# One place for each of the last steps of an RWKV kernel: the order of the last fourteen pairs and last four groups written out

## The chip, the cores and the metric

The kernel runs on one core of one Trainium2 chip. The metric is the device time of one execution in microseconds (us).

## The reference

The reference is the RWKV "wkv" recurrence over `k` and `v` of shape 16 x 2048 x 256 (batch, time, channel), with a decay `w` and a bonus `u` per channel:

```python
for b in range(batch):
    aa = bb = 0;  pp = -1e38
    for t in range(seq_len):
        ww = u + k[b, t];  qq = max(pp, ww)
        e1 = exp(pp - qq);  e2 = exp(ww - qq)
        output[b, t] = (e1 * aa + e2 * v[b, t]) / (e1 * bb + e2 + 1e-08)
        ww = pp - w + k[b, t];  qq = max(ww, k[b, t])
        e1 = exp(ww - qq);  e2 = exp(k[b, t] - qq)
        aa = e1 * aa + e2 * v[b, t];  bb = e1 * bb + e2;  pp = qq
```

So each output is a weighted sum of all earlier values divided by the sum of the weights.

## The kernel before

**Tiling.** Time is cut into 16 groups of 128 steps, and the batch into 4 portions of 4 rows. One *pair* is one portion of one group, a tile of 128 time steps by 4 rows by 256 channels; pair `n` belongs to group `c = n // 4`, and there are 64 pairs. Inside a pair the 128 steps are two halves of 64. The state at the start of each half is carried for a whole group at once.

**What is done for pair n.** Each of these is a *step* with a name:

- `LK`, `LV`: loads of k and v (512 KB each), issued by GpSimd (POOL), the first three pairs by SyncE (SP). `RK` casts k to the matmul's format, `CV` casts v to bf16. `RK` is on VectorE (DVE) for three pairs of four and on POOL for the fourth; `CV` is on POOL from pair 10 on.
- `R q n` and `L q n` (q is 0 or 1): TensorE (PE) matmuls that write decay terms (from `WU`, made of w and u by step `wu`) and then the k term into one of two PSUM tiles `X0`, `X1`. `X q n`: ScalarE (ACT) takes the exponential of the tile into a ring of 11 pairs (`EZR`).
- `TV`: DVE multiplies the exponentials by v. `S`: PE adds up each half's sums into `TOT`.
- `DEN`: PE builds the denominator in an `X` tile. `LN`: ACT takes its logarithm (scaled) into `rd`; `INV`: ACT takes exp(-x) of it in place, which gives the inverse. `NUM`: PE builds the numerator, in its own PSUM tile `num`, and in an `X` tile for odd pairs from 57 on. `MUL`: DVE multiplies both into `ot`. `ST` and `SQ`: stores, on SP and (from pair 52 on, one piece) POOL; the last piece of pair 63 on ACT.

**What is done for group c.** `CS` copies the sums (DVE), `TU` turns them by matmul (PE), `SL` takes logarithms (ACT), `FR` and `OF` make frames and offsets (DVE), `SW` makes weights (ACT), `CH` and `SS` run the recurrence over the halves and spread it (DVE), `TK` turns the states back (PE), `BK` copies them out as `cb` (DVE); `SN` and `KP` hand over to the next group (DVE). `DEN` and `NUM` of the group's pairs need `BK`.

**What sets the order.** Each step gets a *place*, a number: for pair n it is n plus an offset from the table `P` (with separate tables for the last ten pairs' outputs, for the first and the last group's states). `AT` overrides places by name; `mats` makes four small matrices and `wu` the rows of w and u. A loop then takes, again and again, the step with the smallest place whose predecessors (`after`) have been recorded and whose buffer (`take`) is free, and records its instructions:

```python
    todo = sorted(ops, key=lambda x: ops[x]["place"])
    while todo:
        for name in todo:
            o = ops[name]
            if all(x not in ops or "done" in ops[x] for x in o["after"]) and (xs if o["take"] == "X" else free.get(o["take"], 1)):
                break
```

This happens when the program is built; on the chip each engine runs its own instructions in the order in which they were recorded, and waits on semaphores for the others. The two `X` tiles are handed out by the same loop: a step that takes `"X"` (`R`, `DEN`, odd `NUM` at the end) gets the tile that has been free longest. PE also records fillers: `zeros(m)` writes m small matmuls into the tile `TURN` ahead of certain steps (one ahead of each `L`, one ahead of `TU`, four ahead of `TK`; more in the first group). Buffers that count here: 2 of `vb` (from `CV` to `TV`), 2 of `rd` (from `LN` to `MUL`), 1 of `num`, 4 each of `kr` and `vr`, 5 of `kf`, 8 of `ot`.

Of the kernel before, what the change touches and what calls it, by code (L numbers as in the profile page):

```python
# [15 lines left out]
def kernel(  # L16
# [45 lines left out]
         "Z0": {"L": 1, "S": 3, "DEN": 0, "NUM": 6, "TK": 47, "TU": 17, "R": 12},  # L62
         "Z": {"DEN": 0, "L": 1, "NUM": 0, "TK": 4, "S": 0, "TU": 1, "R": 0}}

    AT = {"INV 55": 69.0, "SL 15": 69.1, "LN 56": 69.2, "SW 15": 75.7, "FR 15": 69.3}

    consts = ctx.enter_context(tc.tile_pool(name="consts", bufs=1))
    kpool = ctx.enter_context(tc.tile_pool(name="kpool", bufs=NK))
# [18 lines left out]
    def matrix(name, dt):  # L87
        return consts.tile([128, 128], dt, tag=name, name=name)
# [89 lines left out]
    mats = {name: matrix(name, BF16) for name in ("Id", "IdN", "S", "SN")}  # L178
# [11 lines left out]
    X = [psx.tile([128, 2, D], F32, tag=f"X{a}", name=f"X{a}") for a in range(2)]  # L190
# [31 lines left out]
    AS, D1, L1, A0, FR, BC, A2 = range(7)  # L222
# [88 lines left out]
    RD, NUM, OT = {}, {}, {}  # L311
# [66 lines left out]
    def step(name, place, fn, args=(), after=(), take=None, give=(), mode=0):  # L378
        key = name if isinstance(name, str) else " ".join(map(str, name))
        ops[name] = dict(place=AT.get(key, place), fn=fn, args=args, after=list(after), take=take, give=give, mode=mode)  # L380

# [109 lines left out]
```

## Time and profile before

| | |
|---|---|
| median of 3 runs | 289.46 us (288.67 to 289.91) |
| the profiled execution: time | 289.2 us |
| its span, first to last instruction | 287.5 us |
| busy share of the span | PE 94%, ACT 90%, DVE 86%, POOL 61% |
| granted TensorE clock, mean | 0.995 |
| HBM read and written | 67.12 MB and 33.55 MB, 350 GB/s over the span |

The profile is one execution of the program. Its timeline lists start and duration of instructions per engine in us from the span's start, and in brackets the idle time of the engine before them with what ended it. PEld is the loading of matmul weights. In a group of rows "L210" is line 210 of the kernel; "x4" says that four instructions are merged.

### The profile page before, as it was taken

What the parts mean: (1) busy time and instruction counts of PE and PEld (TensorE: products, weight loads), DVE (VectorE), ACT (ScalarE), POOL (GpSimd) and SP (SyncE); (2) the same over time, 40 slices, a digit from 0 to 9 for tenths busy, and PEclk for the clock granted to TensorE, in tenths of its full rate; (3) what the DMA queues carried; (4) which work ended last, traced back from release to release, by engine and by line L of the source; (5) the groups of instructions that cost most, each with busy time, mean ns of one, the idle gap of its engine ahead of it and who ended that gap; (6) DMA issues with size and microseconds to landing.
All of it is one profiled execution on the core that took longest, in us unless ns stands there. A gap on an engine that the chain in (4) does not pass through costs nothing.

```text
span 287.5 us, 8058 instructions
## 1 busy us (share of the span) xinstructions
PE 271.6 (94%) x3263; PEld 139.2 (48%) x3263; DVE 246.9 (86%) x422; ACT 258.6 (90%) x291; POOL 176.4 (61%) x219
## 2 busy tenths in 40 slices
PE   7989999999999999999999999999999999998860
PEld 6535744454545545454545545454545545454530
DVE  4685879989897979989898989989898989889861
ACT  1776399999999999999999999999999999998991
POOL 8256458575767687575767687575767685421320
PEclk9999999999999999999999999999999999999997
DMA  6999999999999999999999999999999999985896
GB/s 206 348 354 346 347 348 313 384 369 390 374 394 381 383 393 372 391 382 393 355 392 388 389 387 382 394 385 395 370 380 374 389 394 387 347 237 177 235 278 179
DMA packets 58669, 101.20 MB, mean 352 GB/s; under 512 B 5152, under 2 KB 43688, under 8 KB 58632
## 3 DMA queue, kind: packets, MB, share of 16 engines
q0 software_dynamic: 21200, 65.42, 65.5%
q1 hardware_dynamic: 37280, 35.14, 36.4%
q8 instruction: 25, 0.41, 0.6%
q10 hardware_dynamic: 152, 0.14, 0.1%
q14 instruction: 12, 0.10, 0.1%
HBM read 67.12 MB, written 33.55 MB: 350 GB/s over the span
## 4 chain that ended last, share of the span: by engine, by line
PE 81%; ACT 6%; DMA 4%; DVE 4%; issue 2%; SPq 1%; DVEq 0%; ACTq 0%
PE X L207 20%; PE X L323 15%; PE num L323 12%; PE X L201 12%; PE TURN L149 11%; PE TOT L246 7%; DMA ot<-in_v_dram 4%; ACT rd L335 3%; PE TOT L259 2%; DVE ot L355 2%; ACT rd L340 2%; DVE EZR L219 1%; ACT EZR L210 1%; PE TURN L303 1%; SPq L115 1%
## 5 line engine op out<-in xcount | busy, mean ns | idle before, releaser
L210 ACT ACTIVATE EZR<-X 128x1024 bf16<-128x1024 f32 x128 | 126.9, 1014 | 14.4 <-PE X L207 14.2
L214 POOL CAST vb<-vr 128x1024 bf16<-128x1024 f32 x54 | 56.4, 1044 | 69.3 <-DVE EZR L219 67.5
L219 DVE TENSOR_TENSOR EZR<-EZR,vb 128x2048 bf16<-128x2048 bf16 x64 | 77.8, 1219 | 0.4 <-ACT EZR L210 0.2
L355 DVE TENSOR_TENSOR ot<-num,rd 128x1024 f32<-128x1024 f32 x60 | 73.3, 1221 | 3.9 <-ACT rd L340 3.6
L340 ACT ACTIVATE rd<-rd 128x1024 f32<-128x1024 f32 (+1 forms) x65 | 68.0, 1046 | 2.0
L335 ACT ACTIVATE rd<-X 128x1024 f32<-128x1024 f32 (+1 forms) x65 | 65.8, 1012 | 2.3 <-PE X L323 0.7
L149 PE MATMUL TURN<-Z 128*128 128x192 bf16 x319 | 55.2, 259 | 1.4 <-DVE Z L133 1.4
L201 PE MATMUL X<-WU,CO 64*64 64x512 bf16 x512 | 51.9, 390 | 0.9 <-DVE WU L176 0.6
L149 PEld LDWEIGHTS <-Z 128*128 128x128 bf16 x319 | 28.4, 100 | 48.6 <-issue 47.1
L115 POOL DMA_DIRECT2D vr<-in_v_dram x61 | 46.3, 759 | 6.7 <-DVE vb L214 5.9
L207 PE MATMUL X<-kr,NLE 128*128 128x512 f32 x128 | 45.6, 438 | 0.0
L207 PE MATMUL X<-kr,NLZ 128*128 128x512 f32 x128 | 45.5, 437 | 0.0
L108 POOL DMA_DIRECT2D kf<-in_k_dram x53 | 40.1, 756 | 0.0
L194 DVE CAST kr<-kf 128x1024 fp32r<-128x1024 f32 x39 | 31.6, 839 | 4.0 <-DMA kf<-in_k_dram 4.0
L201 PEld LDWEIGHTS <-CO 64*64 64x64 bf16 x512 | 15.7, 105 | 31.1 <-issue 26.3
L323 PE MATMUL X<-EZR,S 64*64 64x512 bf16 x256 | 26.2, 394 | 1.7 <-ACT rd L335 1.0
L323 PE MATMUL X<-cb,Id 64*64 64x512 bf16 x256 | 25.9, 376 | 0.0
L323 PE MATMUL X<-EZR,Id 64*64 64x512 bf16 x256 | 25.9, 376 | 0.0
L323 PE MATMUL num<-EZR,SN 64*64 64x512 bf16 x240 | 24.3, 386 | 1.1 <-DVE ot L355 1.1
L246 PE MATMUL TOT<-EZR,OH 128*32 128x256 bf16 x512 | 23.7, 277 | 1.3 <-DVE EZR L219 1.3
L323 PE MATMUL num<-cb,IdN 64*64 64x512 bf16 x240 | 24.0, 376 | 0.0
L323 PE MATMUL num<-EZR,IdN 64*64 64x512 bf16 x240 | 23.9, 376 | 0.0
(69 smaller groups left out, 269.3 us busy)
## 6 DMA issues: line engine op xcount, KB each, us to landing
vr<-in_v_dram POOLq DMA_DIRECT2D x61, 512.0 KB, 7.7
kf<-in_k_dram POOLq DMA_DIRECT2D x53, 512.0 KB, 8.5
out_dram<-ot SPq DMA_DIRECT2D x64, 256.0 KB, 10.0
out_dram<-ot SPq DMA_DIRECT2D x116, 128.0 KB, 10.1
kr<-in_k_dram POOLq DMA_DIRECT2D x8, 512.0 KB, 8.8
ot<-in_k_dram SPq DMA_DIRECT2D x3, 512.0 KB, 5.9
ot<-in_v_dram SPq DMA_DIRECT2D x3, 512.0 KB, 10.0
out_dram<-ot POOLq DMA_DIRECT2D x11, 128.0 KB, 3.4
```

What stands on the lines that cost most here:

```text
L115: K((SP if n < BYSP else POOL).dma_start(out=vr, in_=rows_of(v, n)))
L149: K(PE.matmul(TURN[:, 0:192], Z[:, 0:128], Z, start=first, stop=True, skip_group_check=True))
L201: K(PE.matmul(X[a][o:o + HS, i, :].rearrange("p (n d) -> p n d", n=2), CO[r:r + HS, q, :], WU[r:r + HS, :].unsqueeze(1).broadcast_to([HS, ...
L207: K(PE.matmul(X[a][:, i, :], (NLE, NLZ)[q], km[:, i, :], start=False, stop=True, skip_group_check=True))
L210: K(SC.activation(ez(n)[:, q, 1], X[a], ACT.Exp))
L214: K((DVE if n < EARLY else POOL).tensor_copy(vb, VR.pop(n)))
L219: K(DVE.tensor_mul(ez(n)[:, :, 0], ez(n)[:, :, 1], vb.unsqueeze(1).broadcast_to([128, 2, 2, D])))
L246: K(PE.matmul(t[32 * j:32 * j + 32, 0:256], OH[:, s:s + 32], ez(n)[:, 0, 1 - q, i, 256 * x:256 * x + 256], start=p == 0 and x == 0, stop=p ...
L323: K(PE.matmul(out_tile[o:o + HS, i, :], left, right, start=s == 0, stop=s == 2, tile_position=(r, o), skip_group_check=True))
L335: K(SC.activation(RD[n][:, i], X[a][:, i], ACT.Ln, scale=RS))
L340: K(SC.activation(RD[n][:, i], RD[n][:, i], ACT.Exp, scale=-1.0))
L355: K(DVE.tensor_mul(o.rearrange("p (i n) d -> p i (n d)", i=2)[:, i], NUM[n][:, i], RD[n][:, i]))
```

## The change

`AT`, which held five places (`INV 55`, `SL 15`, `LN 56`, `SW 15`, `FR 15`), now holds a place for every `R`, `L`, `X`, `TV`, `S`, `DEN`, `LN`, `INV`, `NUM` and `MUL` of pairs 50 to 63, for every state step of groups 12 to 15, and for `mats` and `wu`. Loads, casts and stores (`LK`, `LV`, `RK`, `CV`, `ST`, `SQ`) keep the places that `P` gives, though they can be recorded earlier or later as their predecessors are.

```diff
-    AT = {"INV 55": 69.0, "SL 15": 69.1, "LN 56": 69.2, "SW 15": 75.7, "FR 15": 69.3}
+    AT = {"R 0 50": 48.908, "L 0 50": 39.3462, "X 0 50": 45.2, "R 1 50": 43.3225, "L 1 50": 41.2788,
+          "X 1 50": 48.01, "TV 50": 51.2875, "S 50": 52.283, "DEN 50": 59.8517, "LN 50": 51.2544, "INV 50": 58.126,
...
+          "MUL 63": 73.9425, "mats": -3.08, "wu": -10.79}
```

The instructions are the same in number and kind. What the places come to is an order on each engine. On PE, from the first difference on (fillers left out, order before on the left, after on the right):

```
before                                       after
TK 11 DEN 42 S 50 NUM 42                     TK 11 DEN 42 NUM 42
R,L 53  S 51  DEN 43 NUM 43                  R,L 53  S 50 S 51  DEN 43 NUM 43
R,L 54  TU 12 DEN 44 NUM 44                  R,L 54  TU 12 DEN 44 S 52 S 53 NUM 44
R,L 55  S 52 S 53  DEN 45 NUM 45             R,L 55  DEN 45 NUM 45
R,L 56  TK 12 DEN 46 S 54 NUM 46             R,L 56  TK 12 S 54 DEN 46 NUM 46
R,L 57  S 55  DEN 47 NUM 47                  R,L 57  DEN 47 S 55 NUM 47
R,L 58  TU 13 DEN 48 NUM 48                  R,L 58  TU 13 DEN 48 NUM 48
R,L 59  S 56 S 57  DEN 49 NUM 49             R,L 59  DEN 49 NUM 49
R,L 60  TK 13 DEN 50 S 58 NUM 50             R,L 60  TK 13 DEN 50 DEN 51 S 56 to S 59 NUM 50
R,L 61  S 59  DEN 51 NUM 51                  R,L 61  TU 14 DEN 52 NUM 51
R,L 62  TU 14 DEN 52 NUM 52                  R,L 62  NUM 52
R,L 63  S 60 S 61  DEN 53 DEN 54 NUM 53      R,L 63  DEN 53 DEN 54 NUM 53 S 60 S 61
TK 14 DEN 55 NUM 54 S 62 S 63 TU 15          TK 14 DEN 55 NUM 54 S 62 S 63 TU 15
DEN 56 NUM 55 DEN 57 NUM 56 DEN 58 NUM 57    DEN 56 NUM 55 DEN 57 DEN 58 NUM 56 NUM 57
TK 15 NUM 58 DEN 59 DEN 60 NUM 59 ...        TK 15 DEN 59 NUM 58 NUM 59 DEN 60 ...
```

On ACT, `SW 11` and `SW 13` move ahead of `X 0 51` and `X 0 59`; `LN 51` and `INV 51` move ahead of `X 0 61`; `SW 14` follows `X 1 62`; `SL 15` moves ahead of `INV 55`. On DVE, `TV 53`, `TV 59` and `TV 62` move up to stand right behind `TV 52`, `TV 58` and `TV 61`; `MUL 44` stands ahead of `TV 54`, `CS 14` ahead of `MUL 50`, `TV 63` ahead of `BK 14`, `MUL 56` ahead of `SS 15`; at the start `wu` and `mats` stand ahead of `RK 0` (before: `RK 0`, `wu`, `RK 1`, `RK 2`, `CV 0`, `TV 0`, `CV 1`, `mats`). On POOL, `CV 55` moves ahead of `RK 55`, and `CV 59` ahead of `LK 63`. SP's order is unchanged. From pair 59 on all `DEN`s get `X0` and the odd `NUM`s `X1`.

42 rows, old and new, of the table AT are left out of this document.

## Prediction

> **What bounds the kernel now.** I read the page, then busy time by stage, then ScalarE's (ACT's) waits, then the timelines of the start and the end. Steps are named as in the code: X is the exponential (L210), LN and INV are L335 and L340, R and L the matmuls that fill X (L201, L207), S the sums (L246), DEN and NUM L323, TV L219, MUL L355, CV and RK the casts L214 and L194, and SL, SW, TU, CS, TK, BK, CH, SS the state steps. The page's engine line:
> ```profile
> PE 271.6 (94%) x3263; PEld 139.2 (48%) x3263; DVE 246.9 (86%) x422; ACT 258.6 (90%) x291; POOL 176.4 (61%) x219
> ```
> Two groups of four pairs, and the stage behind them, as windows (us, then busy per engine in the order PE, PEld, DVE, ACT, POOL):
> ```profile
> 212.00:228.00 16.00, 15.96 (x201) 7.98 (x197) 14.70 (x25) 15.75 (x19) 11.36 (x13) 1.00 1.04 382
> 228.00:244.00 16.00, 15.97 (x201) 7.92 (x197) 15.02 (x25) 15.75 (x19) 10.01 (x12) 1.00 1.05 392
> 244.00:260.00 16.00, 15.56 (x207) 7.59 (x200) 13.71 (x24) 15.72 (x19) 4.76 (x5) 1.00 0.91 290
> ```
> PE and ACT are both full: PE has fillers (L149) in its queue, ACT has about 0.25 us of gaps in 16. They are coupled by the two X tiles, since each R, DEN and odd NUM waits for the ACT step that empties its tile. All of ACT's waits that the profile counts:
> ```profile
> ACT EZR L210 <- PE X L207: 14.2, 12, 4.4
> ...
> ACT U L263 <- PE TOT L259: 1.5, 2, 0.8
> ACT rd L335 <- PE X L323: 0.7, 2, 0.5
> ```
> The first row lies before 40 us. Near the end one hole is left, at SL 15 and LN 56:
> ```profile
> 261.88 1.06 ACT L340 ACTIVATE rd<-rd 128x1024 f32<-128x1024 f32 x1
> 263.61 0.28 ACT L263 ACTIVATE U<-TOT 128x128 f32<-128x128 f32 x1 [0.67 <-PE TOT L259]
> 264.40 1.03 ACT L335 ACTIVATE rd<-X 128x1024 f32<-128x1024 f32 x1 [0.51 <-PE X L323]
> ```
> From there ACT starts an LN each 2.00 us until 278.76, and MUL 63 and the last stores follow. The end is thus set by when ACT gets through its queue. The most that any order can win is about 0.4 us in each of the three groups changed (a period is 16.18, from LN 42 at 212.23 to LN 46 at 228.42; the ACT steps placed end to end at the spacings below give 15.7) and some 0.3 of the hole.
>
> **The change, part by part.** No instruction is added or removed; only the order on PE, DVE, ACT and POOL differs, first at the start, then from SW 11 (207.1 us) on. I follow it with spacings, start to start, read from the timeline of 200 to 260 us. PE: R, L, R, L with fillers 2.02, DEN 0.65 (0.77 in front of an S), NUM 0.65, S 0.33 (0.22 before another S), TU 0.62; from the last L to DEN over TK 1.28; a result is there 0.71 after L's start, 0.84 after DEN's. ACT: LN to INV 1.05, INV to next 0.96, X to next 0.91, SW 0.26, SL 0.16. Hand-over 0.05.
>
> *Start.* Making WU and the four small matrices (wu, mats) now stands ahead of RK 0 on DVE:
> ```profile
> 5.07 0.71 DVE L194 CAST kr<-ot 128x1024 fp32r<-128x1024 f32 x1 [0.67 <-DMA ot<-in_k_dram]
> 5.96 0.29 DVE L175 CAST WU<-WUf 128x256 bf16<-128x256 f32 x1 [0.17 <-DMA WUf<-in_u_dram]
> 6.29 0.48 DVE L176 SCALAR_TENSOR_TENSOR WU<-WU,low,WUf 128x256 bf16<-128x256 bf16 x1
> ```
> wu still waits for u (5.96) and ends at 6.77, mats takes 0.74 (its row: 13.79 to 14.53), RK 0 runs from 7.43 to 8.14. L 0 0 starts at 8.19 instead of 7.21, and so PE and ACT run 0.98 late up to S 1. There PE stands anyway, for TV 1 behind v2's transfer:
> ```profile
> 18.13 0.40 PE L246 MATMUL TOT<-EZR,OH 128*32 128x256 bf16 x6 [0.86 <-DVE EZR L219]
> ```
> S 0 would start at 17.75, S 1 at 17.97, still before 18.13: cost 0. The loads k5 to v6, which POOL issues when PE frees a k tile, go 0.98 later, but the DMA runs at 340 to 365 GB/s from 6 to 30 us with transfers queued (k5 is issued at 12.46 and lands at 19.98), so their landings should hold. If this cover were gone, the start costs up to 1.0.
>
> *SW before X (groups 11 and 13).* SW 11 first puts X 0 51 at 206.45 (0.25 late), so DEN 41 starts at 207.51 instead of 207.26, LN 41 at 208.40 (+0.14), LN 42 at 212.39 (+0.16). S 50, moved behind L 1 53, then lets that L end 0.3 earlier, X 1 53 no longer waits, and LN 43 comes at 216.35 (before 216.36): sum 0.
>
> *Sums.* S 52 and S 53 move ahead of NUM 44: NUM 44 at 220.74 (220.09), X 0 55 at 222.52, DEN 45, which waits for that X, and LN 45 +0.14. S 54 moves from behind DEN 46 to ahead of it:
> ```profile
> 227.13 0.39 PE L303 MATMUL TURN<-Id,CB 128*128 128x128 bf16 x4
> 227.53 0.41 PE L323 MATMUL X<-EZR,S 64*64 64x512 bf16 x4
> ...
> 228.30 0.40 PE L246 MATMUL TOT<-EZR,OH 128*32 128x256 bf16 x8
> ```
> LN 46 hangs on DEN 46, so it comes at 228.79 (228.42, +0.37). S 55 moves behind DEN 47, which waits for X 0 57 (ends 231.81): PE stands 0.6 and does S 55 afterwards. NUM 47 comes 0.64 late, LN 48 at 237.18 (236.53, +0.65). SW 13 ahead of X 0 59 holds DEN 49 to 240.51: LN 49 at 241.40 (+0.77), LN 50 at 245.40 (+0.80).
>
> *DEN 51 directly behind DEN 50.* ACT does LN 50 and LN 51 in one run while PE does S 56 to S 59; the waits before X 1 61 (0.1) and LN 51 (0.2) go. SL 14 comes at 251.24; before, the same set of ACT steps ended at 250.76: +0.48. L 0 63 and L 1 63 then come a little late: X 1 63 at 256.66 (255.92, +0.74).
>
> *Tail.* From X 1 63: LN 53 257.58, INV 53 258.63, MUL 53 259.72, TV 63 (now ahead of BK 14) 260.86, S 63 262.13, CS 15 262.59, TU 15 263.07, SL 15 263.79. SL 15 now stands ahead of INV 55, so ACT idles 1.2 in one place, not 0.67 and 0.51 in two. LN 56 at 264.91 (+0.51), LN 57 267.04. LN 58 waited for MUL 56 (268.64); MUL 56, now ahead of SS 15, ends at 268.75, before ACT is ready: LN 58 at 269.05 (268.74, +0.31). All DENs from 59 on share one X tile; each starts 0.05 after the LN that frees it and is done 0.84 later, in the 0.98 that INV takes: still 2.00 per pair. Stores follow unchanged.
>
> *Casts.* TV 53 now directly follows TV 52, so POOL's CV 54 (waits for TV 52's end) runs beside it; CV 55 comes ahead of RK 55 and waits for v55 (landed 219.18). What a collision costs:
> ```profile
> 216.90 1.04 POOL L214 CAST vb<-vr 128x1024 bf16<-128x1024 f32 x1 [0.52 <-DVE EZR L219]
> 217.88 1.50 POOL L194 CAST kr<-kf 128x1024 fp32r<-128x1024 f32 x1
> ```
> RK 55 took 1.50 beside DVE's RK 56 (0.99); alone the two kinds take 1.04 and 0.68. So CV 55 ends near 220.25 and RK 55 between 221.3 (alone) and 221.75; L 0 55 would start at 221.77. If CV 55 too is stretched by 0.46, PE waits 0.45. Bounds 0 to 0.45, and I take 0.15, nearer to the row with one stretch. LK 58, LV 57 and LK 59 go 2 us later; their data had 3.4 us and more to spare before first use.
>
> **Sum.** 0 + 0.31 + 0.15 = +0.45 us. The profiled execution took 289.20 (span 287.5 and 1.7 around it): 289.65; the median of the runs lies 0.26 higher, so 289.9.
>
> **Rivals.** *POOL's casts against TV (slower).* If CV 54 (216.90) gets ahead of TV 53 (216.75) and holds it for its 1.04, TV 53 ends at 219.15, CS 12 starts at 219.06, TU 12 at 219.55 (218.80), MUL 43 ends between 221.6 and 222.05, and NUM 44 comes 0.9 to 1.35 late, on PE and not hidden. With 0.31: +1.2 to +1.65, near 291.1; with v55 another 0.8 late, 291.9. For it: stretched casts are in the trace. Against: TV 53 should be first by 0.15. It decides at which of the two starts first. The Trainium skill (SBUF — State Buffer, "Who interferes with whom") says that a VectorE op with two SBUF inputs and a GpSimd op that reads SBUF exclude each other for the whole instruction; by it the later one loses the full duration, not the 0.3 to 0.5 of the rows. The stretches agree with it, and no row shows a TV beside a POOL cast.
>
> *Start not covered (slower).* TV 1 or the landings slip too: +0.31 and +1.0, near 290.8 to 290.9. Against it: 0.16 us of slack by the rows above.
>
> *The sums cost nothing (faster).* If ACT runs end to end through the three groups, 1.2 is won there and 0.2 to 0.3 at LN 58: 288.0 to 288.3. For it: fewer waits at LN 51 and LN 58. Against it: PE is as full as ACT, and S 54 stands in front of a DEN on which ACT waits already.
>
> **Chances.** Forecast 0.42, POOL's casts 0.35, start 0.09, sums free 0.14. Counting 0.5% (1.45 us, about what a measurement of this kernel can tell from no change): slower 0.31 from the casts, 0.04 from the start, 0.03 from the forecast's upper edge, 0.38; faster 0.08, from the low half of the last case; same 0.54. The range leaves out about 0.1 on each side: 288.2 to 291.9; the forecast's own range is 289.5 to 290.3.
>
> **What would show it.** Right: LN 43 near 216.4 and then LN 46, LN 48 and LN 50 later by 0.4, 0.7 and 0.8; PE idle before DEN 47 and DEN 49; ACT idle over 1 us at SL 15; S 1 again at 18.1. Wrong: S 1 later than 18.2 (start), TV 53 starting after 217 or L 0 55 after 222 (casts), X 1 63 before 255.9 (sums free), or LNs further apart than 2.00 in the tail (the one X tile).

## The result and the profile after

The changed kernel takes 291.00 us (median of 17 runs, 289.86 to 291.76), the kernel before 289.46 in the same job (17 runs, 288.60 to 290.06). The ratio is 1.0044, 95% interval 1.0031 to 1.0057: 1.27 us longer (0.90 to 1.65). The two medians lie 1.54 apart, inside that interval; the ratio is what this text goes by, here and for every experiment. The profiled execution, 289.86 us with a span of 288.1, is the lowest of the 17, so the trace alone shows less than the loss: 0.66 us against the profiled execution before.

In the changed kernel every line number is 44 higher (X is L254, LN and INV L379 and L384, R and L L245 and L251, S L290, DEN and NUM L367, TV L263, MUL L399, CV and RK L258 and L238, SL L307). The engine line of its page, and the three windows shown of before (columns as there, the DMA share and GB/s last):
```profile
PE 271.4 (94%) x3263; PEld 140.3 (49%) x3263; DVE 248.8 (86%) x422; ACT 258.8 (90%) x291; POOL 177.8 (62%) x219
```
```profile
212.00:228.00 16.00, 15.65 (x199) 8.23 (x193) 15.83 (x24) 15.45 (x19) 11.86 (x13) 1.00 1.04 354
228.00:244.00 16.00, 14.81 (x174) 6.92 (x166) 14.48 (x25) 15.50 (x18) 9.16 (x12) 1.00 1.04 391
244.00:260.00 16.00, 15.66 (x214) 8.28 (x214) 13.42 (x24) 15.84 (x19) 7.09 (x6) 1.00 0.80 275
```
ACT's busy time falls from 15.75 to 15.45 and 15.50 in the first two windows and rises from 15.72 to 15.84 in the third. So ACT has about 0.3 us more of gaps in each of the two groups where the S move, and 0.1 less in the one where DEN 51 joins DEN 50. PE, which was full, now stands 0.35 and 1.2 (S 56 and S 57, 0.65 of work, have moved from the second window to the third).

ACT's waits, and the hole near the end, as they are after:
```profile
ACT EZR L254 <- PE X L251: 14.4, 13, 5.3
...
ACT U L307 <- PE TOT L303: 2.0, 2, 1.2
ACT rd L379 <- PE X L367: 0.3, 2, 0.2
```
```profile
261.79 1.01 ACT L379 ACTIVATE rd<-X 128x1024 f32<-128x1024 f32 x1
263.98 0.28 ACT L307 ACTIVATE U<-TOT 128x128 f32<-128x128 f32 x1 [1.18 <-PE TOT L303]
264.15 1.05 ACT L384 ACTIVATE rd<-rd 128x1024 f32<-128x1024 f32 x1
265.10 1.02 ACT L379 ACTIVATE rd<-X 128x1024 f32<-128x1024 f32 x1
```
The two holes of 0.67 and 0.51 have become one of 1.18 at SL 15, and LN 56 starts at 265.10 (264.40).

The trace can be cut at ACT's steps. LN 40 (204.17 before, 204.24 after) stands ahead of every moved step but the start's. From there:

| stretch | before | after | change | predicted |
|---|---|---|---|---|
| LN 40 to LN 42 | 8.06 | 8.19 | +0.13 | +0.16 |
| LN 42 to LN 44 | 8.12 | 7.95 | -0.17 | -0.16 |
| LN 44 to LN 46 | 8.07 | 8.72 | +0.65 | +0.37, casts +0.15 |
| LN 46 to LN 48 | 8.11 | 8.31 | +0.20 | +0.28 |
| LN 48 to LN 50 | 8.07 | 8.19 | +0.12 | +0.15 |
| LN 50 to X 1 63 | 11.32 | 11.22 | -0.10 | -0.06 |
| X 1 63 to LN 56 | 8.48 | 8.28 | -0.20 | -0.23 |
| LN 56 to LN 58 | 4.34 | 4.13 | -0.21 | -0.20 |
| LN 58 to the end of INV 63 | 12.41 | 12.39 | -0.02 | 0 |
| sum | 76.98 | 77.38 | +0.40 | +0.46 |

On ACT's path of this execution the sum was right to 0.06. The runs are longer by 1.27. The experiments ask for the other 0.9 (1.27 less 0.40), and whether the terms above are what the blocks of the change cost.

### The profile page after: what moved, and what is told of

It reads as the page before. It is cut to its first block, busy times and chain, and to the rows that moved or that the text cites. A ratio compares the mean times of both kernels' runs of the same rounds, so it can differ in the third digit from the quotient of the medians.

```text
span 288.1 us, 8060 instructions
## 1 busy us (share of the span) xinstructions
PE 271.4 (94%) x3263; PEld 140.3 (49%) x3263; DVE 248.8 (86%) x422; ACT 258.8 (90%) x291; POOL 177.8 (62%) x219
## 4 chain that ended last, share of the span: by engine, by line
PE 72%; ACT 17%; DVE 4%; issue 2%; DMA 1%; POOL 0%; DVEq 0%; POOLq 0%
PE X L251 18%; PE X L367 14%; PE num L367 11%; PE TURN L193 11%; PE X L245 10%; ACT rd L379 6%; PE TOT L290 6%; ACT EZR L254 5%; ACT rd L384 5%; PE TOT L303 2%; DVE ot L399 1%; DMA WUf<-in_u_dram 1%; DVE EZR L263 1%; PE TURN L347 1%; DVE kr L238 1%
## 5 line engine op out<-in xcount | busy, mean ns | idle before, releaser
L254 ACT ACTIVATE EZR<-X 128x1024 bf16<-128x1024 f32 x128 | 126.5, 1014 | 14.5 <-PE X L251 14.4
L258 POOL CAST vb<-vr 128x1024 bf16<-128x1024 f32 x54 | 59.1, 1096 | 69.6 <-DVE EZR L263 67.1
L399 DVE TENSOR_TENSOR ot<-num,rd 128x1024 f32<-128x1024 f32 x60 | 73.2, 1220 | 5.9 <-ACT rd L384 3.3
L263 DVE TENSOR_TENSOR EZR<-EZR,vb 128x2048 bf16<-128x2048 bf16 x64 | 77.5, 1218 | 0.4 <-ACT EZR L254 0.2
L384 ACT ACTIVATE rd<-rd 128x1024 f32<-128x1024 f32 (+1 forms) x65 | 68.0, 1046 | 2.0
L379 ACT ACTIVATE rd<-X 128x1024 f32<-128x1024 f32 (+1 forms) x65 | 65.7, 1011 | 2.0 <-PE X L367 0.3
L245 PE MATMUL X<-WU,CO 64*64 64x512 bf16 x512 | 51.9, 390 | 0.5 <-DVE WU L220 0.2
L251 PE MATMUL X<-kr,NLE 128*128 128x512 f32 x128 | 45.6, 438 | 0.8 <-DVE kr L238 0.8
L251 PE MATMUL X<-kr,NLZ 128*128 128x512 f32 x128 | 45.5, 437 | 0.0
L238 DVE CAST kr<-kf 128x1024 fp32r<-128x1024 f32 x39 | 32.8, 870 | 4.5 <-DMA kf<-in_k_dram 4.5
L245 PEld LDWEIGHTS <-CO 64*64 64x64 bf16 x512 | 15.9, 104 | 30.8 <-issue 25.8
L367 PE MATMUL X<-EZR,S 64*64 64x512 bf16 x256 | 26.2, 395 | 4.0 <-ACT rd L379 2.0
L367 PE MATMUL X<-cb,Id 64*64 64x512 bf16 x256 | 25.9, 376 | 0.0
L367 PE MATMUL X<-EZR,Id 64*64 64x512 bf16 x256 | 25.9, 375 | 0.0
L367 PE MATMUL num<-EZR,SN 64*64 64x512 bf16 x240 | 24.3, 385 | 0.5 <-DVE ot L399 0.4
L367 PE MATMUL num<-cb,IdN 64*64 64x512 bf16 x240 | 24.0, 376 | 0.0
L367 PE MATMUL num<-EZR,IdN 64*64 64x512 bf16 x240 | 24.0, 376 | 0.0
L290 PE MATMUL TOT<-EZR,OH 128*32 128x256 bf16 x512 | 22.6, 276 | 0.2 <-ACT U L307 0.2
```

What stands on the lines that cost most here:

```text
L245: K(PE.matmul(X[a][o:o + HS, i, :].rearrange("p (n d) -> p n d", n=2), CO[r:r + HS, q, :], WU[r:r + HS, :].unsqueeze(1).broadcast_to([HS, ...
L251: K(PE.matmul(X[a][:, i, :], (NLE, NLZ)[q], km[:, i, :], start=False, stop=True, skip_group_check=True))
L254: K(SC.activation(ez(n)[:, q, 1], X[a], ACT.Exp))
L258: K((DVE if n < EARLY else POOL).tensor_copy(vb, VR.pop(n)))
L263: K(DVE.tensor_mul(ez(n)[:, :, 0], ez(n)[:, :, 1], vb.unsqueeze(1).broadcast_to([128, 2, 2, D])))
L367: K(PE.matmul(out_tile[o:o + HS, i, :], left, right, start=s == 0, stop=s == 2, tile_position=(r, o), skip_group_check=True))
```

## Experiments: the start and two blocks

Theories. 1: the order of pairs 50 to 63 on PE and ACT costs what the table shows, and the start nothing. 2: the start isn't covered in most executions. 3: the loss is made by the casts and at S 52 and S 53. Orders are shown as lists of steps on one engine.

**The change without its start.**
```diff
 DVE, changed kernel
-wu  mats  RK 0  RK 1  RK 2  CV 0  TV 0  CV 1
+RK 0  wu  RK 1  RK 2  CV 0  TV 0  CV 1  mats
```


> The change without its start: WU and the four small matrices are made after RK 0 and after CV 1 again, everything from pair 50 on as changed. The changed kernel took 1.0044 of the time before. Theory 1 (the start costs nothing, the whole loss lies in the order of pairs 50 to 63): 1.0040 to 1.0050, about 290.7 on a kernel before of 289.46. Theory 2 (in most executions the start is not covered and costs 0.7 to 1.0 us; the profiled execution of the changed kernel was one with an early v2): 1.0010 to 1.0020, about 289.9.

Measured: 1.0039 (1.0023 to 1.0054). That is theory 1's time: without its start the kernel is 0.15 us faster, give or take 0.59, so a start of 0.7 to 1.0 is ruled out, but not one of half that. The trace says more. PE's timeline at S 0 and S 1 (L290) and the R behind them, of the changed kernel:
```profile
17.66 0.62 PE L290 MATMUL TOT<-EZR,OH 128*32 128x256 bf16 x16
18.21 0.41 PE L245 MATMUL X<-WU,CO 64*64 64x512 bf16 x4
```
and of this one:
```profile
17.01 0.39 PE L290 MATMUL TOT<-EZR,OH 128*32 128x256 bf16 x8
17.34 0.41 PE L245 MATMUL X<-WU,CO 64*64 64x512 bf16 x4
```
Before, S 1 stood 0.86 for TV 1 and this R came at 18.46. With the same start it comes at 17.34 here, and nothing waits: v2 landed earlier (TV 1 at 15.41, before 16.86).

**The changed start alone, in the kernel before.** The same two lines of DVE's list, the other way round.

> The kernel before with the changed start alone. Theory 1: 1.0000, within 0.1%, and S 1 at 18.1 us as before. Theory 2: 1.0025 to 1.0035, 290.2 to 290.5, with S 1, L 0 5 and all that follows later by what the end is later. Both theories want the same S 1 if v2 lands at 16.25 us as in the profile before; they differ where v2 lands earlier.

Measured: 1.0026 (1.0008 to 1.0043), 0.75 us longer. S 0 and S 1 run from 17.99 without a wait and R follows at 18.55. Theory 1 fails, since 1.0000 lies outside the interval: the start does cost.

**S 52, S 53, TV 53 and CV 55 back.**
```diff
 PE, changed kernel
-R,L 54  TU 12  DEN 44  S 52 S 53  NUM 44  R,L 55  DEN 45
+R,L 54  TU 12  DEN 44  NUM 44  R,L 55  S 52 S 53  DEN 45
 DVE
-TV 52  TV 53  CS 12  RK 56  MUL 43  FR 12  OF 12  SN 12
+TV 52  CS 12  RK 56  MUL 43  FR 12  OF 12  SN 12  TV 53
 POOL
-CV 54  CV 55  RK 55
+CV 54  RK 55
```


> The changed kernel with one block undone: TV 53 behind SN 12 again, CV 55 behind RK 55 and its loads, S 52 and S 53 behind L 1 55. Theory 1 (S 52 and S 53 ahead of NUM 44 cost 0.14, the casts 0.15): 0.3 us less than the changed kernel, 1.0034, LN 46 near 228.7. Theory 3 (casts and the S 52 that waits cost all that LN 45 is late, 0.53): 0.5 us less, 1.0027, LN 45 near 224.45. If the block pays for itself later (TV 53 early relieves VectorE): no less, 1.0044.

Measured: 1.0043 (1.0028 to 1.0058). LN 44 to LN 45 takes 4.09 as before (changed kernel 4.59), but LN 45 to LN 46 takes 4.48 (4.13), so that LN 46 gains only 0.15. From LN 40 to the end of INV 63 it is 77.24: 0.14 is won, less than theory 3 wants. In the runs nothing is won (0.03 us, give or take 0.57), as if the block paid for itself later; that interval doesn't rule out theory 1's 0.3 or theory 3's 0.5.

**S 54, S 55, DEN 47 and TV 54 back.**
```diff
 PE, changed kernel
-R,L 56  TK 12  S 54  DEN 46  NUM 46  R,L 57  DEN 47  S 55  NUM 47
+R,L 56  TK 12  DEN 46  S 54  NUM 46  R,L 57  S 55  DEN 47  NUM 47
```


> The changed kernel with another block undone: TV 54 behind SS 12 again, S 54 behind DEN 46, S 55 ahead of DEN 47. Theory 1 (these two places cost 0.37 and 0.28 at LN 46 and LN 48): 0.4 to 0.6 us less than the changed kernel, 1.0025 to 1.0030, LN 46 near 228.8 and LN 48 near 236.8. Theory 3 (the loss is made at pairs 52 and 53 and by the casts): 1.0040, LN 48 no earlier than 237.2.

Measured: 1.0015 (0.9996 to 1.0033), with 77.04 from LN 40 to the end of INV 63: 0.34 won in the trace, 0.84 in the runs (give or take 0.65). LN 44 to LN 46 takes 8.55, LN 46 to LN 48 takes 8.12. So the two blocks overlap: S 52 and S 53 alone make LN 46 late by 0.48, S 54 alone by 0.50, both by 0.65. The 0.20 at LN 48 comes with this block alone (S 55 behind DEN 47).

**The same block alone, in the kernel before.** DVE has TV 54 ahead of CH 12, PE has S 54 ahead of DEN 46 and DEN 47 ahead of S 55.

> The kernel before with one block of the change alone: TV 54 ahead of CH 12, S 54 ahead of DEN 46, DEN 47 ahead of S 55. From the profile of the changed kernel with and without this block: LN 46 0.4 to 0.5 late, LN 48 0.6 to 0.7 late, LN 63 about as much, since nothing behind it gives back: 1.0022. If the block costs what undoing it seemed to win in the timed runs (0.0029 of the time, 0.8 us): 1.0030. If it costs only beside S 52 and S 53: 1.0000 to 1.0010.

Measured: 1.0011 (0.9992 to 1.0030), which tells the block neither from nothing nor from the 0.8 us that undoing it won. The trace has LN 44 to LN 46 at 8.55 (+0.48), LN 46 to LN 48 at 8.32 (+0.21) and nothing given back behind it: 77.65, which is 0.67 longer. ACT's timeline shows the first of the two, at LN 46:
```profile
225.96 1.92 ACT L254 ACTIVATE EZR<-X 128x1024 bf16<-128x1024 f32 x2
228.40 1.03 ACT L379 ACTIVATE rd<-X 128x1024 f32<-128x1024 f32 x1 [0.52 <-PE X L367]
```
ACT has done X 0 56 and X 1 56 and stands 0.52 for DEN 46, which comes behind S 54.

**A cast against SS 12.** Two of the three profiles with the whole changed order from pair 50 to 57 (the one without the start and the one with NUM 58 early, below) have LN 44 to LN 46 at 9.11 and 9.18, and not 8.72. TV 54 ahead of CH 12 brings SS 12 (L340) down beside CV 56. In the changed kernel's profile SS 12 starts first; DVE, then POOL:
```profile
226.80 0.33 DVE L340 TENSOR_TENSOR CB<-AB,G 128x128 bf16<-128x128 f32 x1
```
```profile
227.01 1.05 POOL L258 CAST vb<-vr 128x1024 bf16<-128x1024 f32 x1
```
In the kernel without the start CV 56 is first by 0.05; DVE, POOL, and PE at TK 12:
```profile
226.40 1.20 DVE L340 TENSOR_TENSOR CB<-AB,G 128x128 bf16<-128x128 f32 x1
```
```profile
226.35 1.05 POOL L258 CAST vb<-vr 128x1024 bf16<-128x1024 f32 x1
```
```profile
227.65 0.40 PE L347 MATMUL TURN<-Id,CB 128*128 128x128 bf16 x4 [0.22 <-DVE CB L340]
```
SS 12 then ends 0.20 behind the cast and takes 1.20 and not 0.33, PE waits for it, and LN 46 comes 0.39 later (0.46 in the other kernel). In the two other kernels with TV 54 ahead of CH 12, SS 12 is first by 0.03 and takes 0.33: a few hundredths decide. With the block undone SS 12 starts 4.91 after LN 44, 1.5 ahead of CV 56. So on top of the other block this one costs 0.34 where SS 12 wins and about 0.75 where it loses, which is nearer to the 0.84 of the runs. What brings the two so close is the first scan of CH 12: it takes 1.08 and not 0.36 in all five kernels with TV 54 ahead of CH 12, while POOL only issues loads; why, the runs don't show.

## Experiments: one step in the tail

Cutting the traces left a step that the prediction hadn't priced: NUM 58, which the change puts behind DEN 59. DEN 59 waits for LN 58; NUM 58 waits for nothing of the kind, but now stands behind it. DVE's timeline at MUL 57, BK 15, MUL 58 and MUL 59, before:
```profile
268.66 1.22 DVE L355 TENSOR_TENSOR ot<-X,rd 128x1024 f32<-128x1024 f32 x1
269.80 0.68 DVE L307 CAST cb<-TURN 128x512 bf16<-128x512 f32 x1
270.88 1.23 DVE L355 TENSOR_TENSOR ot<-num,rd 128x1024 f32<-128x1024 f32 x1 [0.40 <-ACT rd L340]
272.89 1.22 DVE L355 TENSOR_TENSOR ot<-X,rd 128x1024 f32<-128x1024 f32 x1 [0.78 <-ACT rd L340]
```
and after:
```profile
269.35 1.22 DVE L399 TENSOR_TENSOR ot<-X,rd 128x1024 f32<-128x1024 f32 x1
270.49 0.68 DVE L351 CAST cb<-TURN 128x512 bf16<-128x512 f32 x1
271.88 1.23 DVE L399 TENSOR_TENSOR ot<-num,rd 128x1024 f32<-128x1024 f32 x1 [0.70 <-ACT rd L384]
273.35 1.23 DVE L399 TENSOR_TENSOR ot<-X,rd 128x1024 f32<-128x1024 f32 x1 [0.25 <-ACT rd L384]
```
MUL 58 is 1.00 late and MUL 59 0.46, so two pairs' stores are issued 1.47 apart and not 2.01. (The profile names ACT for MUL 58's wait, but INV 58 had ended near 271.3; NUM 58 ended at 271.77.) That matters only if the DMA can't catch up. The windows of the tail, before:
```profile
270.00:276.00 6.00, 4.46 (x76) 2.46 (x72) 4.04 (x4) 5.90 (x7) 1.83 (x3) 1.00 0.94 270
276.00:282.00 6.00, 2.80 (x48) 1.40 (x40) 3.87 (x5) 5.05 (x7) 1.82 (x3) 1.00 0.92 270
```
and after:
```profile
270.00:276.00 6.00, 5.18 (x84) 2.85 (x84) 4.27 (x5) 5.91 (x7) 1.82 (x3) 1.00 0.90 255
276.00:282.00 6.00, 2.98 (x48) 1.54 (x47) 3.99 (x5) 5.49 (x8) 1.81 (x3) 1.00 0.95 277
```
A pair's 0.52 MB in 2.0 us are 262 GB/s, and with the 16 DMA engines 90 to 95% busy they move 255 to 277. Theory 4: what is bunched there stays in the queue to the last store. Its rival is that the end of the stores only varies from execution to execution.

**The changed kernel with NUM 58 early.**
```diff
 PE, changed kernel
-TK 15  DEN 59  NUM 58  NUM 59  DEN 60
+TK 15  NUM 58  DEN 59  NUM 59  DEN 60
```


> The changed kernel with NUM 58 ahead of DEN 59 again. In the profile of the changed kernel MUL 58 starts at 271.88, 1.0 later than before, while MUL 59 is 0.46 later; the last store then lands 4.33 us after its issue, before 3.92, and a kernel with the changed start alone 3.65. Theory 4 (two stores bunched at pairs 58 and 59 leave a queue of stores that the last four pairs cannot work off, since these write one pair in 2.0 us at 94% of what the DMA does): MUL 58 near 271.3, LN 63 unchanged, the last store 3.5 to 3.9 after its issue, the time 0.4 to 0.6 us under the changed kernel, 1.0025 to 1.0030 of before. Rival (what the end of the stores takes varies by itself): 1.0044, and the last landing anywhere from 3.6 to 5.0.

Measured: 1.0036 (1.0023 to 1.0049), 0.23 us under the changed kernel, give or take 0.53. MUL 58 follows LN 58 by 2.12 (changed kernel 2.65), and MUL 59 follows MUL 58 by 2.05, as meant. The last store lands 4.14 after its issue, not 3.5 to 3.9. This tells nothing apart.

**The kernel before with NUM 58 late.**
```diff
 PE, kernel before
-NUM 57  TK 15  NUM 58  DEN 59  DEN 60
+NUM 57  TK 15  DEN 59  NUM 58  DEN 60
```


> The kernel before with this one step moved: NUM 58 behind DEN 59. NUM 58 ends near 271.3 and MUL 58 starts 0.4 to 0.5 late; LN 58 to LN 63 and MUL 59 to MUL 63 stay where they are. Theory 4: 0.4 to 0.5 us longer, 1.0015, the last store landing 4.1 to 4.4 after its issue. Rival: 1.0000.

Measured: 1.0044 (1.0029 to 1.0059; 6 runs), 1.27 us longer, nearly three times what theory 4 expected. Yet from LN 40 to the end of INV 63 its trace has 76.98, the kernel before to the hundredth, and MUL 59 to MUL 63 keep their places behind LN 58. The one step costs as much as the whole change, and in this trace none of it on the path of PE, ACT and DVE behind LN 40.

**Both, without the stores of pair 60.** First the control, the kernel before with those three stores left out:
```diff
-        step(("ST", n), place("ST"), store, (n,), ...
+        step(("ST", n), place("ST"), store if n != 60 else (lambda n: None), (n,), ...
-            step(("SQ", n), place("SQ"), store_rest, (n,), ...
+            step(("SQ", n), place("SQ"), store_rest if n != 60 else (lambda n: None), (n,), ...
```


> The kernel before with the three stores of pair 60 left out (those rows of the output are not written): 0.52 MB less in the queue of the last four pairs. It is the control of the run that follows. If a queue of stores is still there at the end of the kernel before (its last store lands 3.95 us after MUL 63 ends, and the stores of pairs 55 and 56, ahead of the crowd, take 3.0 to 3.5 from issue): last landing 3.2 to 3.5 after MUL 63, 0.4 to 0.7 us shorter, 0.9980. If a store simply takes that long: 1.0000 and 3.7 to 4.0.

Measured: 0.9983 (0.9964 to 1.0002), with the last landing 3.68 after MUL 63's end, not the 3.2 to 3.5 expected of a queue that is gone. Then the same edit with NUM 58 late:

> NUM 58 behind DEN 59 in the kernel before (which alone took 1.0044, with the last landing 4.99 after MUL 63), and the stores of pair 60 left out (those rows of the output are not written). Theory 4 (the late MUL 58 costs by a queue of stores that lasts to the end): with 2.0 us of stores taken out the queue is gone, so the same time as the control without these stores, within 0.1%, and the last landing 3.2 to 3.5 after MUL 63. If NUM 58 costs in another way (PE or ACT): still 0.4% longer than the control.

Measured: 0.9974 (0.9957 to 0.9992). It isn't longer than its control, but 0.26 us shorter, give or take 0.75; with the stores in, the late NUM 58 made 1.27. The two differ by 1.53, give or take 0.86. MUL 58 and MUL 59 are 1.48 apart here too. The last store (the one on ACT's queue; the last column is us from issue to landing) in the kernel with NUM 58 late:
```profile
out_dram<-ot ACTq DMA_DIRECT2D x1, 128.0 KB, 5.0
```
and in the kernel with NUM 58 late and pair 60's stores left out:
```profile
out_dram<-ot ACTq DMA_DIRECT2D x1, 128.0 KB, 3.6
```
The control without them has 3.6 too. The window that follows (columns as above), in the kernel with NUM 58 late, first with those stores and then without:
```profile
276.00:282.00 6.00, 3.04 (x52) 1.54 (x47) 3.99 (x5) 5.78 (x8) 1.81 (x3) 1.00 0.94 276
276.00:282.00 6.00, 3.50 (x60) 1.67 (x51) 4.29 (x4) 5.87 (x9) 1.21 (x3) 1.00 0.68 193
```
With the DMA 0.68 busy (0.67 in the control) there is room to work off what was bunched. So this pair of pairs shows that the cost of the late NUM 58 in the kernel before goes through the stores, as theory 4 says: take 2.0 us of writing out, and no cost is seen. It doesn't show the size. MUL 58 is 0.52 late (2.67 behind LN 58, before 2.15). If the stores behind it went out at the same rate as before, they could be no later than that, and the runs say 0.84 at least. What makes it more stays open. Single traces don't help: the profile with NUM 58 late spans 1.8 us more than that of before, but PE stops in it for 0.66 at NUM 36 behind a late k tile, far ahead of the step that moved. The last landing after MUL 63's end is 4.36, 4.50, 5.04, 3.93 and 4.99 us in five kernels with NUM 58 late, and 3.95, 3.68, 4.17, 3.76, 3.86, 4.75 and 5.60 in seven with it early. That varies more from execution to execution than the effect is large, so only repeated runs can tell.

## Experiments: the part that gains

**The kernel before with the changed order from DEN 51 on.** NUM 58 is early; on DVE and ACT the moves from TV 59 and LN 51 on are kept.
```diff
 PE, kernel before
-TK 13  DEN 50  S 58  NUM 50  R,L 61  S 59  DEN 51  NUM 51  R,L 62
+TK 13  DEN 50  DEN 51  S 56 S 57 S 58 S 59  NUM 50  R,L 61
...
-DEN 57  NUM 56  DEN 58  NUM 57  TK 15  NUM 58  DEN 59  DEN 60  NUM 59
+DEN 57  DEN 58  NUM 56  NUM 57  TK 15  NUM 58  DEN 59  NUM 59  DEN 60
 DVE
-MUL 53  BK 14  TV 63      CH 15  SS 15  MUL 56
+MUL 53  TV 63  BK 14      CH 15  MUL 56  SS 15
```


> The kernel before up to pair 50 (its start, its SW 11 and SW 13, its S 50 to S 55 and DEN 47, its TV 53 and TV 54, its casts) and the changed order from DEN 51 on, with NUM 58 ahead of DEN 59. From the stretches of the profiles so far: LN 50 to X 1 63 0.10 shorter, X 1 63 to LN 56 0.20, LN 56 to LN 58 0.21, so LN 63 0.5 earlier than before if the part up to LN 50 is as before. All theories on order: 0.9980 to 0.9985, 288.8 to 288.9. If the stores of the last pairs set the end and not ACT: 1.0000.

Measured: 0.9970 (0.9955 to 0.9985), 288.81 us: faster than both kernels. From LN 40 to the end of INV 63 it takes 76.52, 0.46 less than before.

**The same with the changed start.**

> The same with the changed start. It differs from the one before it by the start alone. Theory 1 (covered by v2 in TV 1): no difference. Theory 2 (not covered in most executions; what is left of it behind the next loads is 0.25 to 0.5, from LN 8 at 74.18 without the start and 74.44 to 74.85 with it): 0.3 to 0.5 us longer than the kernel without the start, 1.0000 of before.

Measured: 0.9986 (0.9974 to 0.9998). The start costs 0.16%, 0.46 us (give or take 0.56), here. Together with the 0.75 of the start alone and the 0.15 between the changed kernel and that without its start, weighted by their intervals, it is 0.48 us, give or take 0.32.

**INV 55 ahead of SL 15 as well.**

> The late part of the change with NUM 58 early (0.9970 so far), and INV 55 ahead of SL 15 as in the kernel before. SL 15 waits 1.18 us for TU 15; INV 55 takes 1.05 and fits in. LN 56 then waits for DEN 56, which ends 0.74 after SL 15 starts: LN 56 0.32 earlier, and SW 15, CH 15, MUL 56 and LN 58 to LN 63 with it. 0.3 us less if ACT sets the end: 0.9960. If the stores do, or LN 58 stands behind MUL 56 all the same: 0.9970.

Measured: 0.9967 (0.9949 to 0.9985), 288.72 us. ACT's timeline has INV 55 in the hole, no wait at SL 15, and half a microsecond in front of LN 56:
```profile
261.73 1.06 ACT L384 ACTIVATE rd<-rd 128x1024 f32<-128x1024 f32 x1
262.88 0.28 ACT L307 ACTIVATE U<-TOT 128x128 f32<-128x128 f32 x1
263.66 1.03 ACT L379 ACTIVATE rd<-X 128x1024 f32<-128x1024 f32 x1 [0.50 <-PE X L367]
```
LN 56 comes 0.33 earlier behind LN 55, but LN 58 to LN 59 takes 2.13 and no longer 2.03, and the 76.29 from LN 40 to the end of INV 63 is 0.23 less than without the step. In the runs it is 0.1 us, far inside their intervals.

## Why the prediction was right or wrong

Forecast: 289.9 us, within 0.5% of before, with 289.5 to 290.3 as the forecast's own range. Measured: 291.00 us, 0.44% longer with an interval that reaches past 0.5%, 1.27 us and not 0.45, above the forecast's own range and inside the whole one (288.2 to 291.9). It lies inside because that range spans the rivals too. Two terms set at nothing were wrong, one size was, and a collision came where none was looked for. That the sum fits ACT's path of the one profile to 0.06 is partly luck: the 0.15 for the casts stood in for a wait of S 52, and SS 12 happened to win there (0.40; 0.78 and 0.93 in the two profiles where it lost).

*Start, set at 0: wrong, 0.3 to 0.5.* L 0 0 starts at 8.08, 0.87 late, and S 1's last matmuls come no later than before, as predicted. The cover was real in the profile of before and absent in most other profiles. The R behind S 1 starts when PE gets there or about 1.6 after TV 1 starts, whichever is later. With the old start eight profiles have it at 17.32 to 18.49, mean 17.81 (five of them by 17.8); with the new one six have it at 18.21 to 18.55, mean 18.40. Half is given back by LN 8 (mean 74.43 and 74.72), so the traces say 0.30 and the runs 0.48. The rival that priced this at 1.0 had the mechanism, and hung it on one sign (S 1 later than 18.2) that can't show it: that mark itself moves with v2's landing.

*Stores "follow unchanged": wrong.* The step that failed is in the tail. It was followed to LN 58 by the order of the DENs, and NUM 58 behind DEN 59 was read off the list but not carried through MUL 58 to the stores. What it costs the changed kernel the runs can't tell from nothing (0.23, give or take 0.53); on the kernel before it is 1.27, give or take 0.43.

*S 52 and S 53 ahead of NUM 44: mechanism right, size off.* LN 45 comes 0.50 later behind LN 44 (4.59 against 4.09), forecast 0.14. PE's timeline shows the part that was missing:
```profile
220.56 0.62 PE L290 MATMUL TOT<-EZR,OH 128*32 128x256 bf16 x16 [0.24 <-ACT U L307]
221.11 0.41 PE L367 MATMUL num<-EZR,SN 64*64 64x512 bf16 x4
221.35 0.39 PE L367 MATMUL num<-EZR,IdN 64*64 64x512 bf16 x4
221.56 0.39 PE L367 MATMUL num<-cb,IdN 64*64 64x512 bf16 x4
221.78 0.39 PE L245 MATMUL X<-WU,CO 64*64 64x512 bf16 x4
222.14 0.72 PE L251 MATMUL X<-kr,NLE 128*128 128x512 f32 x2
```
S 52 writes the tile that TU 12 has filled, and must wait until SL 12 has read it; before, it came after R,L 55 and that was long past. NUM 44 starts at 221.11 (predicted 220.74) and X 0 55 at 222.89 (222.52), both 0.37 later than forecast.

*S 54 and S 55: mechanism right, sizes near.* S 54 alone makes 0.48 to 0.50 at LN 46, where the prediction had 0.37 for it and the block above together; the two together make 0.65, and 0.20 more at LN 48 (predicted 0.28). PE stands 0.56 and 0.55 ahead of DEN 47 and DEN 49, as predicted.

*SW 11, SW 13, DEN 51, the tail's LNs: right*, each within 0.05 (the table). ACT's one hole of 1.2 came as predicted, and the LNs of the tail follow each other at 2.00.

*Casts against TV: not at TV 53, but at SS 12.* The rival's number was near (291.1). At the place it named POOL has CV 54, CV 55 and RK 55, and DVE has TV 52 and TV 53 in one row:
```profile
217.10 1.97 POOL L258 CAST vb<-vr 128x1024 bf16<-128x1024 f32 x1 [0.53 <-DVE EZR L263]
219.85 1.04 POOL L258 CAST vb<-vr 128x1024 bf16<-128x1024 f32 x1 [0.78 <-DMA vr<-in_v_dram]
220.83 1.04 POOL L238 CAST kr<-kf 128x1024 fp32r<-128x1024 f32 x1
```
```profile
215.82 2.35 DVE L263 TENSOR_TENSOR EZR<-EZR,vb 128x2048 bf16<-128x2048 bf16 x2
```
TV 53 was first and took no longer than alone; the cast lost, with 1.97 and not 1.04, and ended 0.90 after TV 53. CV 55 then stood for v55, and RK 55 ended at 221.88 (221.3 to 221.75 predicted). L 0 55 at 222.14 came straight behind R 0 55, so S 52's wait hid the casts; without it they would have cost some 0.15 (an estimate from these times). The prediction's sign for this rival, L 0 55 after 222, was thus met for another reason. The rival's mechanism, a DVE step that starts just behind a POOL cast and loses its whole time, turned up later, at SS 12, and cost 0.39 and 0.46 where it struck. The prediction followed the casts of v54 and v55 and not that of v56.

The Trainium skill (SBUF — State Buffer, "Who interferes with whom") states that the port pair which VectorE shares with GpSimd is an exclusive lock, that a VectorE instruction with two SBUF inputs contends for it with a GpSimd instruction that reads SBUF, and that the order of issue decides which of them blocks. Both places agree: 0.93 lost by the cast, 0.87 by SS 12. The rows used in the prediction would have made it 0.46, so the whole duration, which the prediction drew from that section, was the better guide.

Put together, the terms are start +0.30 (by LN 8), ACT's path from LN 40 to the end of INV 63 as the traces have it, and +0.27 for a late NUM 58. For the changed kernel the path is the mean over the three profiles with its order (0.40, 0.78, 0.93: 0.70), and 0.27 is what is left of 1.27. The start alone has the path of before, since a late load stopped PE in its profile. Against the runs, in us:

| kernel | start | path | NUM 58 | sum | measured |
|---|---|---|---|---|---|
| changed | 0.30 | 0.70 | 0.27 | 1.27 | 1.27 (set) |
| without its start | 0 | 0.70 | 0.27 | 0.97 | 1.13 ± 0.45 |
| start alone | 0.30 | 0 | 0 | 0.30 | 0.75 ± 0.51 |
| S 52 block back | 0.30 | 0.26 | 0.27 | 0.83 | 1.24 ± 0.43 |
| S 54 block back | 0.30 | 0.06 | 0.27 | 0.63 | 0.43 ± 0.54 |
| NUM 58 early | 0.30 | 0.70 | 0 | 1.00 | 1.04 ± 0.38 |
| NUM 58 late alone | 0 | 0 | 0.27 | 0.27 | 1.27 ± 0.43 |
| S 54 block alone | 0 | 0.67 | 0 | 0.67 | 0.32 ± 0.55 |
| late part | 0 | -0.46 | 0 | -0.46 | -0.87 ± 0.43 |
| late part and start | 0.30 | -0.48 | 0 | -0.18 | -0.41 ± 0.35 |
| late part, INV 55 | 0 | -0.69 | 0 | -0.69 | -0.96 ± 0.52 |

All but one lie within their intervals, three of them barely (start alone, S 52 block back, late part), and the first fits by its making. NUM 58 late alone costs at least 0.57 more than the table gives it. That this cost goes through the stores is shown there; why it is so large, and why the same step should cost the changed kernel so much less, stays open, as does the share of the changed kernel's executions in which SS 12 loses. So 0.27 is a remainder, and no run shows it as NUM 58's.

## What to carry to other kernels

A moved step is followed until its last consumer, its stores too: one matmul step behind another's wait cost the kernel before 1.27 us (0.84 at least) through its stores, with ACT's path unchanged to a hundredth in the trace. A wait that covers an added cost has to be there in every execution; one profile shows a transfer's landing once, and a price set at nothing on its strength needs the other case in the sum. And the part of a reordering that wins should be run by itself: here it gives 0.9970, while the whole gave 1.0044.

## What the runs showed that was not expected

Landings vary by more than the change is worth. TV 1, behind v2's cast on DVE, starts between 15.39 and 16.91 in fourteen profiles. In the steady part, where the DMA's busy share is 1.04 and 1.05 at 382 and 392 GB/s (kernel before, 212 to 244 us), a late k tile stops PE for 0.36 to 0.66 in some executions, not always at the same pair (seen behind RK 32, 40, 44, 48, 56 and 60). The changed kernel's profile has one of these on DVE, RK 32 in front of MUL 19, which delays NUM 20 and so PE:
```profile
120.65 1.46 DVE L238 CAST kr<-kf 128x1024 fp32r<-128x1024 f32 x1 [0.85 <-DMA kf<-in_k_dram]
122.03 1.21 DVE L399 TENSOR_TENSOR ot<-num,rd 128x1024 f32<-128x1024 f32 x1
```
From LN 20 to LN 26 it takes 24.60 where the kernel before took 24.25. The profile of before has no such stop, nor has that of the late part alone; the twelve others have one to three. That, v2 and the stores' end (3.7 to 5.6 us behind MUL 63) go into the 1.0 to 2.5 us between the lowest and the highest run of one kernel.
